# A decoder layer on one core: P3 summed onto P5, block-transposed norm roots, and a separate pool for the gate operand

## The chip, the cores and the metric

The kernel runs on one core of a Trainium2 chip. The metric is the time of one execution in microseconds (us) on the device, as the median of several runs. Engines are named as the profile names them: PE is TensorE's matmul (PEld its weight load), DVE VectorE, ACT ScalarE, POOL GpSimd, SP SyncE, whose queue issues most transfers.

## The reference

One decoder layer, batch 1, 1024 tokens of 1024 features, all in fp32:

```python
z = rms_norm(h, norm_mix_g)            # n0
proj = z @ w_in                        # pool, LRU and gate channels
h = h + concat(pool_mixer, rg_lru * gelu(gate)) @ w_out
z = rms_norm(h, norm_mlp_g)            # n1
h = h + square(relu(z @ w_up)) @ w_down        # 4096 hidden
z = rms_norm(h, norm_ple_g)            # n2
gate = sigmoid(z @ w_ple_gate + b_ple_gate)
h = h + gate * (p @ w_ple_proj)        # p: 256 features
return rms_norm(h, norm_final_g)       # fin
```

## The kernel before, in words

**Layout and precision.** Activations lie transposed: features on the 128 partitions, tokens along the row. A tile of 128x1024 is one block of 128 features. A product of fp32 accuracy is made of three matmuls: each operand is split into an upper part (a cast to `float32r`, on ACT, line 153) and a lower part (the value less the upper part, on DVE, line 154; with a norm gain lines 156 and 157), and `mm` (line 321) issues upper x upper, upper x lower and lower x upper into one PSUM bank. So every weight tile goes through a load, an ACT cast and a DVE subtraction before its matmuls, and one weight pair of tiles (`wu_0` ... `wu_3`, `wd_P_0` ... in the rows) is made while another is used.

**Stages.** Up to 155 us: first norm, input projection, mixers and gates. To 242: output projection (`ps_o`). To 557: MLP up (`ps_P_u`), 16 pairs of row blocks; the two blocks of a pair and the two halves of the tokens form a 2x2 block product that is done in seven products P1 to P7 in place of eight; POOL and DVE make the sums of weights that these need (lines 183 and 186), DVE adds the results (`add`, line 652). To 863: MLP down (`ps_P_d`) in the same way, 14 products of four quarters q. Then the gated embedding: a gate product (`ps_e`, 24 matmuls a tile) and a projection of p (`ps_j`, 6 matmuls) for eight feature tiles and three token groups, 0 to 511, 512 to 767 and 768 to 1023, and the final norm of each group with its store.

**Norms.** A norm adds up squares on DVE (line 355) into an accumulator. `sums` splits that into two parts on DVE (cast line 367, subtraction line 368, tile `hl` or `ple`), and a matmul with a matrix of ones adds over partitions, so each partition of `n_ps` holds the sums for all tokens. `roots` takes the square root of it on ACT (line 384), and a DVE reciprocal of 128x512 follows (line 402; for n1 lines 749 and 754, inside pair 1). `rstd_fast`, used in the final norm only, transposes 32x32 blocks on DVE instead (line 391), takes the root and the reciprocal of the few distinct values (128x16 or 128x8, lines 395 and 396), and transposes back (line 397). n1 belongs to the first up pair, `up_first`, in which P6, P7, P4 and P5 run before P1, P2 and P3; its `sums` stand at P3. The gain by R is applied in `finish_up` (line 665), one pair late. n2 belongs to the last products of MLP down (P5, P3); its sums and the splits of the gate operand Z (line 157, tile `ple`) are made around 854 to 864.

**What sets the order.** The code is written in one sequence; a scheduler reorders instructions of each engine, except those wrapped in `pin`, which keep program order. Tiles come from pools that are opened and closed by `space` and `leave`; a tile in a pool's place waits for all users of the pool before. PSUM products alternate between a pool `pd` of single banks and `pp` of double ones (`turn` counts). Loads are issued on SP's queue in order, except that of the input projection's first weight tile (`wl`, k = 0), which is on ACT's.

**The end.** In the last group of 256 tokens the last tile's product is followed by a sigmoid (ACT, line 933), a multiplication (DVE, line 941), an addition (942), a square (1010), the ones-matmul (379), the root and reciprocal between transpositions, seven multiplications and one scaling of 128x256 (lines 964 and 968), and four stores of two tiles each. `outT` has a row of 1024 tokens per feature, so a packet of these stores holds 256 tokens.

Of the kernel before, what the change touches and what calls it, by code (L numbers as in the profile page):

```python
# [12 lines left out]
P = 128  # L13
# [10 lines left out]
LAST_POOL = ()  # L24
# [26 lines left out]
def block_kernel(  # L51
# [14 lines left out]
    outT: bass.AP,  # L66
# [193 lines left out]
    def down_step(c, kind, q):  # L260
# [22 lines left out]
        (load_weights, w_lru[k * P : (k + 1) * P, :], f"wl{k}", 3 * P, None, nc.sync if k else nc.scalar)  # L283
# [27 lines left out]
    def mm(parts, whi, wlo, zhi, zlo, first, last, only=None):  # L311
# [7 lines left out]
        for w, z in ((whi, zhi), (whi, zlo), (wlo, zhi)):  # L319
            for hs, ps in outs:  # L320
                nc.tensor.matmul(  # L321
                    ps, w, z[:, hs],
                    start=first and z is zhi and w is whi,
                    stop=last and w is wlo,
                )

# [13 lines left out]
    class Norm:  # L340


        def __init__(self, name, acc, tmp, eng=None, late=()):
            self.name, self.acc, self.tmp, self.late = name, acc, tmp, late
# [13 lines left out]
        def sums(self, halves=HALVES):  # L358

            parts = []  # L360
            for hs in halves:
                n = hs.stop - hs.start
                j = (hs.start // HALF) % 2
                hi, lo = hl(2 * j)[:, :n], hl(2 * j + 1)[:, :n]
                o = bank(f"{self.name}_ps{hs.start}")[:, :n]
                in_order[:] = self.late
                pin(nc.vector.tensor_copy(hi, self.acc[:, hs]))
                pin(nc.vector.tensor_tensor(lo, self.acc[:, hs], f32(hi), ALU.subtract))
# [13 lines left out]
        def roots(self, out, parts):  # L382
            for hs, o in parts:
                nc.scalar.activation(out[:, hs], o, AF.Sqrt, bias=eps, scale=1.0 / D)

        def rstd_fast(self, out, parts):


            for hs, o in parts:
# [213 lines left out]
    norm = Norm("n1", T[4], T[5:], late=[True])  # L603
# [41 lines left out]
    def product(ps, w, operand, ts=range(4), n=4):  # L645
        (whi, wlo) = w
        for t in ts:
            zhi, zlo = operand(t)
            mm([(FIRST, ps)], kblk(whi, t), kblk(wlo, t), zhi, zlo, t == 0, t == n - 1)
# [49 lines left out]
    def up_first():  # L699
# [388 lines left out]
```

## Time and profile before

| | |
|---|---|
| median of 3 runs | 990.07 us (989.76 to 990.35) |
| profiled execution | 988.36 us, span 986.5 us |
| instructions | 11505, matmuls 4472 |
| PE busy | 968.2 us (98%) |
| DVE, ACT, POOL busy | 775.0, 445.8, 100.4 us |
| granted TensorE clock | 0.995 of full speed over the span |

A row of the timeline starts with its start in us from the start of the span and its duration, then the engine, the line of the kernel, the operation, output and inputs, the shape and how many such rows are merged; in brackets stands the engine's idle time before it and what ended that. In a stretch of time (A:B) stand busy times with counts in the order PE, PEld, DVE, ACT, POOL, then the granted clock, the share of DMA engines in use and GB/s.

### The profile page before, as it was taken

The page shows a single profiled execution, that of the slowest core. Times are in us where ns is not written, and L with a number is a line of the kernel's source. Part 1 is how long each engine was busy: PE and PEld are TensorE (multiplying, and loading weights), DVE is VectorE, ACT ScalarE, POOL GpSimd, SP SyncE. Part 2 cuts the span into 40 slices and gives each one's busy share as a digit, 9 for nine tenths or more (in the row PEclk, how much of TensorE's full clock was granted, in tenths as well). Part 3 has the DMA queues.
Part 4 walks back from the last instruction along what each step waited for, and adds up shares of the span by engine and source line. Part 5 has one row for each costly group of instructions (what it writes and reads, how often), then busy time and mean ns, then how long its engine had stood idle before and what let it go on. Part 6 is the DMA issues. An engine that isn't in the chain of part 4 may idle for free.

```text
span 986.5 us, 11505 instructions
## 1 busy us (share of the span) xinstructions
PE 968.2 (98%) x4472; PEld 805.6 (82%) x4472; DVE 775.0 (79%) x883; ACT 445.8 (45%) x526; POOL 100.4 (10%) x72
## 2 busy tenths in 40 slices
PE   9999999999899999999999999999999999999996
PEld 7888888888677888888888888888888888878995
DVE  7999994459896777767767889879775668795976
ACT  8368743347333334333433444344343335653544
POOL 0000000002522332232232000000000000000110
PEclk9999999999999999999999999999999999999998
DMA  6210243112124533543543897356533331131122
GB/s 223 88 44 33 86 150 107 44 43 71 47 108 155 196 118 139 199 133 126 175 169 118 293 359 261 132 174 208 175 117 95 107 106 44 43 111 61 44 86 86
DMA packets 46710, 125.04 MB, mean 127 GB/s; under 512 B 5312, under 2 KB 8384, under 8 KB 46656
## 3 DMA queue, kind: packets, MB, share of 16 engines
q1 hardware_dynamic: 46368, 124.08, 36.8%
q8 instruction: 35, 0.57, 0.2%
q10 hardware_dynamic: 288, 0.24, 0.1%
q14 instruction: 19, 0.16, 0.0%
HBM read 90.74 MB, written 33.55 MB: 126 GB/s over the span
## 4 chain that ended last, share of the span: by engine, by line
PE 84%; DVE 9%; ACT 3%; DMA 1%; issue 1%; SPq 1%; POOL 1%; DVEq 0%; ACTq 0%; POOLq 0%
PE ps_P_d L321 30%; PE ps_P_u L321 28%; PE ps_i L321 10%; PE ps_o L321 8%; PE ps_e L321 5%; PE ps_l L321 1%; PE ps_g L321 1%; DVE t L355 1%; DVE h L942 1%; DVE h L955 1%; DVE wu_lo L154 1%; DVE y L157 1%; DVE t L941 1%; SPq L419 1%; DMA h<-in_xT 1%
## 5 line engine op out<-in xcount | busy, mean ns | idle before, releaser
L321 PE MATMUL ps_P_d<-a,wd_P_hi 128*128 128x512 f32 x880 | 271.0, 389 | 0.0
L321 PEld LDWEIGHTS ps_P_d<-a,wd_P_hi 128*128 128x128 f32 x880 | 165.2, 188 | 34.5
L321 PE MATMUL ps_P_d<-a,wd_P_lo 128*128 128x512 f32 x440 | 171.3, 389 | 0.0
L321 PE MATMUL ps_P_u<-a,wu_hi 128*128 128x512 f32 x512 | 157.7, 389 | 0.0
L321 PE MATMUL ps_P_u<-y,wu_hi 128*128 128x512 f32 x384 | 119.1, 392 | 0.0
L321 PEld LDWEIGHTS ps_P_u<-a,wu_hi 128*128 128x128 f32 x512 | 96.1, 188 | 20.0
L652 DVE TENSOR_TENSOR t<-t,ps_P_u 128x512 f32<-128x512 f32 (+1 forms) x84 | 65.1, 779 | 46.5 <-PE ps_P_u L321 45.8
L321 PE MATMUL ps_P_u<-a,wu_lo 128*128 128x512 f32 x256 | 99.6, 389 | 0.0
L321 PEld LDWEIGHTS ps_P_d<-a,wd_P_lo 128*128 128x128 f32 x440 | 82.6, 188 | 17.3 <-DVE wd_P_lo L154 0.3
L321 PEld LDWEIGHTS ps_P_u<-y,wu_hi 128*128 128x128 f32 x384 | 72.6, 189 | 15.2 <-ACT wu_hi L153 0.2
L321 PE MATMUL ps_P_u<-y,wu_lo 128*128 128x512 f32 x192 | 75.3, 393 | 3.4 <-DVE wu_lo L154 3.4
L321 PE MATMUL ps_i<-a,wi_hi 128*128 128x512 f32 x288 | 77.5, 390 | 0.0
L154 DVE TENSOR_TENSOR a<-wd,a 128x1024 fp32r<-128x1024 f32 x56 | 67.1, 1219 | 6.4 <-ACT a L153 5.3
L153 ACT ACTIVATE a<-wd 128x1024 fp32r<-128x1024 f32 x56 | 58.8, 1057 | 22.3 <-PE ps_P_d L321 11.8
L321 PE MATMUL ps_o<-y,wo_hi 128*128 128x512 f32 x256 | 68.4, 389 | 0.0
L321 PEld LDWEIGHTS ps_i<-a,wi_hi 128*128 128x128 f32 x288 | 53.9, 188 | 11.5 <-ACT h L520 0.5
L153 ACT ACTIVATE wu_hi<-wu 128x1024 fp32r<-128x1024 f32 x24 | 25.5, 1062 | 82.9 <-PE ps_P_u L321 45.8
L153 ACT ACTIVATE wu_hi<-wu_raw 128x1024 fp32r<-128x1024 f32 (+1 forms) x25 | 25.3, 1010 | 74.9 <-PE ps_P_u L321 37.5
L321 PEld LDWEIGHTS ps_o<-y,wo_hi 128*128 128x128 f32 x256 | 48.0, 188 | 10.0
L321 PEld LDWEIGHTS ps_P_u<-a,wu_lo 128*128 128x128 f32 x256 | 48.0, 188 | 10.0
L154 POOL TENSOR_TENSOR wg_lo<-wg_raw,wg_hi 128x1024 fp32r<-128x1024 f32 x4 | 9.7, 2436 | 410.3 <-ACT wg_hi L153 410.3
L153 ACT ACTIVATE wd_P_hi<-wd 128x1024 fp32r<-128x1024 f32 x24 | 25.4, 1059 | 56.4 <-PE ps_P_d L321 56.2
(225 smaller groups left out, 1655.8 us busy)
## 6 DMA issues: line engine op xcount, KB each, us to landing
wd<-act SPq DMA_DIRECT2D x56, 512.0 KB, 5.6
act<-t SPq DMA_DIRECT2D x32, 512.0 KB, 3.9
wu_raw<-in_w_up SPq DMA_DIRECT2D x16, 512.0 KB, 4.2
wu<-in_w_up SPq DMA_DIRECT2D x16, 512.0 KB, 4.2
act<-wu SPq DMA_DIRECT2D x16, 512.0 KB, 4.2
wd<-in_w_down SPq DMA_DIRECT2D x16, 512.0 KB, 6.2
h<-in_xT SPq DMA_DIRECT2D x15, 512.0 KB, 4.5
wg_raw<-in_w_gate SPq DMA_DIRECT2D x12, 512.0 KB, 3.3
```

Of the source, the lines that this page charges most:

```text
L153: pin(nc.scalar.activation(hi, src, AF.Copy))
L154: pin((eng or nc.vector).tensor_tensor(lo, src, f32(hi), ALU.subtract))
L157: pin(nc.vector.scalar_tensor_tensor(lo, src, g, f32(hi), ALU.mult, ALU.subtract))
L321: nc.tensor.matmul(ps, w, z[:, hs], start=first and z is zhi and w is whi, stop=last and w is wlo,)
L355: self.eng.tensor_tensor(self.acc[:, hs], self.acc[:, hs], sq, ALU.add)
L419: nc.sync.dma_start(rv[r, pair, a, :, r], gates[pair, a, par])
L652: (eng or nc.vector).tensor_tensor(to, to if y is None else y, x, ALU.add)
L941: nc.vector.tensor_tensor(e, t, pj, ALU.mult)
L942: nc.vector.tensor_tensor(hv, hv, e, ALU.add)
L955: nc.vector.scalar_tensor_tensor(hv, hv, col("g_fin", o), rfin[:, hs], ALU.mult, ALU.mult)
```

## The change

1. `up_first`: P3 is summed in PSUM onto the bank that holds P5 (`more=True`: no start flag), after ACT has copied P5 to `s`. The additions on DVE are regrouped: six instead of nine.
2. n1's split is made right after that copy: upper parts on ACT, lower ones on DVE, pinned (`casts`); the four ones-matmuls follow P3 without a product between them.
3. `rstd` is now what `rstd_fast` was, for all norms; the 128x512 reciprocals are gone.
4. `open_down`/`open_ple`/`open_proj`: the second group of down weight tiles has a pool of its own, so that the pool of the gate operand Z can open in P5; the projection's operands have a pool `proj`, and `w_proj` is loaded right behind p on SP's queue. n2's first half is cast at P3 and summed after the first gate.
5. The load of the input projection's first weight tile goes to SP's queue as the others do. In SP's new order the load of the sixth (k = 5) stands ahead of eight small loads (`in_gates`), behind which it stood before.
6. The end: the last tile gets two single PSUM banks; its sigmoid comes before the square and gain of the tile before it; the last two gains are done on ACT; four multiplications of 128x512 write to T[1:3], and the output of the last 256 tokens is stored apart, contiguous in each partition, and put together on the host.

```diff
-        (load_weights, w_lru[k * P : (k + 1) * P, :], f"wl{k}", 3 * P, None, nc.sync if k else nc.scalar)
+        (load_weights, w_lru[k * P : (k + 1) * P, :], f"wl{k}", 3 * P)
...
+        def casts(self, halves=HALVES):
+            for hs in halves:
+                hi, lo = self.parts(hs)
+                nc.scalar.activation(hi, self.acc[:, hs], AF.Copy)
+                ins = nc.vector.tensor_tensor(lo, self.acc[:, hs], f32(hi), ALU.subtract)
+                tc.keep_in_program_order(ins)
...
+        def rstd(self, out, parts=None):
+            for hs, o in parts or self.sums():
                 r = out[:, hs]
                 nc.vector.transpose(r, o)
...
-        def rstd(self, out, parts=None):
-            for hs, o in parts or self.sums():
-                self.roots(out, [(hs, o)])
-                nc.vector.reciprocal(out[:, hs], out[:, hs])
...
-        copy(s, ps["P6"])
-        add(c22, ps["P7"], s)
-        add(c21, ps["P4"], c22)
-        add(c22, ps["P5"])
-        add(c12, ps["P5"], s)
+        copy(s, ps["P5"])
+        norm.casts()
...
+        for kind in ("P1", "P2"):
+            ps[kind] = mlp_bank(f"ps_{kind}_u0")
+            product(ps[kind], ws[kind], lambda t, kind=kind: up_operand(kind, t))
+        product(ps["P5"], ws["P3"], lambda t: up_operand("P3", t), more=True)
+        parts = norm.sums(cast=True)
+        copy(c11, ps["P1"])
+        add(c12, ps["P6"], c11)
+        add(c22, ps["P7"], c12)
+        add(c11, ps["P2"])
+        add(c21, ps["P4"], c22)
+        add(c22, s)
+        add(c12, ps["P5"])
+        norm.rstd(R, parts)
...
-            nc.vector.reciprocal(R[:, FIRST], R[:, FIRST])
...
-            nc.vector.reciprocal(R[:, SECOND], R[:, SECOND])
...
-        tiles = space("wd", 12, F32)
+        tiles = space("wd", 8, F32)
+        late = space("wd1", 4, F32, "right")
...
-        tiles = space("ple", 14, F32R)
+        tiles = space("ple", 10, F32R)
...
+        leave("wd1")
         leave("wu")
-        B[2:4] = pairs(space("proj", 4, F32R, "right"))
+        B[:4] = pairs(space("proj", 8, F32R, "right"))
...
                 if n == 0:
+                    first_sums()
                     continue
...
-        for n, o in enumerate(tiles):
-            hv = H[o][:, hs]
-            eng = nc.gpsimd if n in LAST_POOL else nc.vector
-            eng.tensor_tensor(hv, hv, rfin[:, hs], ALU.mult)
+        gain(end, hs)
+        done = t_all[:, 1:3].rearrange("p a (b s) -> p (a b) s", s=hs.stop - hs.start)
+        r = rfin[:, hs].unsqueeze(1).broadcast_to([P, 2, hs.stop - hs.start])
+        low = end // 2 * 2
+        for o in [*(o for o in range(0, NT, 2) if o != low), low]:
+            os = slice(o, o + 2)
+            nc.vector.tensor_tensor(done[:, os], h_all[:, os, hs], r, ALU.mult)
+            nc.sync.dma_start(out_end[:, os], done[:, os])
```

The scheduler decides what these edits do to each engine's order. Three places show it. The first is DVE's queue around the end of `up_first` and the start of pair 1. `hl` is n1's split, `wu_k_lo` the lower part of the up weights' k-th tile, `t<-t,ps_P_u` an addition of a product's result. Before:

```order
L154 TENSOR_TENSOR wu_3_lo<-wu_0_raw,wu_3_hi 128x512
L652 TENSOR_TENSOR t<-t,ps_P_u_1851 128x512 x3
L652 TENSOR_TENSOR t<-t,ps_P_u_1868 128x512
L154 TENSOR_TENSOR wu_0_lo<-wu_1745,wu_0_hi 128x1024
L367 CAST hl_135<-t 128x512
L368 TENSOR_TENSOR hl_135<-t,hl_135 128x512
L367 CAST hl_136<-t 128x512
L652 TENSOR_TENSOR t<-t,ps_P_u_1882 128x512
L368 TENSOR_TENSOR hl_136<-t,hl_136 128x512
L154 TENSOR_TENSOR wu_1_lo<-wu_1745,wu_1_hi 128x1024
L749 RECIPROCAL rstd<-rstd 128x512
L652 TENSOR_TENSOR t<-t,ps_P_u_1932 128x512
```

And now, from the weight part whose product was late at 254.44 (`wu_2_lo`; before, two additions stood ahead of it):

```order
L153 TENSOR_TENSOR wu_2_lo<-wu_0_raw,wu_2_hi 128x1024
L371 TENSOR_TENSOR hl_135<-t,hl_135 128x512
L371 TENSOR_TENSOR hl_136<-t,hl_136 128x512
L153 TENSOR_TENSOR wu_3_lo<-wu_0_raw,wu_3_hi 128x512
L659 TENSOR_TENSOR t<-t,ps_P_u_1783 128x512
L659 TENSOR_TENSOR t<-t,ps_P_u_1793 128x512
L659 TENSOR_TENSOR t<-t,ps_P_u_1808 128x512
L659 TENSOR_TENSOR t<-t,ps_P_u_1868 128x512
L153 TENSOR_TENSOR wu_0_lo<-wu_1749,wu_0_hi 128x1024
L659 TENSOR_TENSOR t<-t 128x512
L659 TENSOR_TENSOR t<-t,ps_P_u_1818 128x512
L402 STREAM_TRANSPOSE rstd<-n_ps_1893 128x512
```

The lower parts of `hl` have moved ahead of all additions, and no cast of the upper parts is left on DVE. Behind these rows follow a second transposition, pair 1's `wu_1_lo`, two reciprocals of 128x16, two transpositions back, the scaling of `up_first`'s result (128x2048), an addition and pair 1's `wu_2_lo`.

The second place is PE at the start of the gated embedding, where n2's sums (`n_ps`) stand. Before, where `ps_P_d_3` is the last down product:

```order
L321 MATMUL ps_P_d_3_5900<-a,wd_P_3_lo 128x512
L321 MATMUL ps_e_0_5939<-ple_5690,wg_0_hi 128x512
L321 MATMUL ps_e_0_5939<-ple_5691,wg_0_hi 128x512
L321 MATMUL ps_e_2_6029<-ple_5698,proj_5930 128x512
L321 MATMUL ps_e_2_6029<-ple_5699,proj_5930 128x512
L370 MATMUL n_ps_5887<-ple_5688,ones 128x512
L321 MATMUL ps_e_1_5970<-ple_5690,wg_1_hi 128x512
```

And now, at the end of the first gate's 24 matmuls:

```order
L320 MATMUL ps_e_0_5942<-ple_5704,wg_0_hi 128x512
L320 MATMUL ps_e_0_5942<-ple_5703,wg_0_lo 128x512
L384 MATMUL n_ps_5974<-ple_5705,ones 128x512
L385 MATMUL n_ps_5974<-ple_5705,ones 128x512
L320 MATMUL ps_e_1_5981<-ple_5697,wg_1_hi 128x512
L320 MATMUL ps_e_1_5981<-ple_5698,wg_1_hi 128x512
```

The lower part's sum came four matmuls into the embedding; both sums now come after a whole gate. DVE's splits of the gate operand, eight in a row before, now stand among the weight parts of the last P5 and P3 products: four, three and one between one part and the next.

The third is ACT at the end, from the last but one sigmoid (`ps_e_2`) on. Before:

```order
L933 ACTIVATE t<-ps_e_2_6913,vecs 128x256
L1012 ACTIVATE t<-h 128x256
L1015 ACTIVATE h<-h,vecs 128x256
L933 ACTIVATE t<-ps_e_3_6955,vecs 128x256
L939 ACT_TABLE_LOAD
L939 ACTIVATE root<-t 128x1
L395 ACTIVATE edge<-t,eps 128x8
```

And now:

```order
L944 ACTIVATE t<-ps_e_2_6925,vecs 128x256
L944 ACTIVATE t<-ps_e_3_6966,vecs 128x256
L1030 ACTIVATE t<-h 128x256
L1031 ACT_TABLE_LOAD
L1031 ACTIVATE root<-t 128x1
L973 ACTIVATE h<-h,vecs 128x256 x2
L406 ACTIVATE edge<-t,eps 128x8
```

The last sigmoid has moved ahead of the square, and two gains now stand between the table load and the root.

More of the change, by code (lines that the diff above doesn't have):

```diff
@@ L309, in small_weights, with mm @@
         return hi, lo
-    def mm(parts, whi, wlo, zhi, zlo, first, last, only=None):
+    def mm(parts, whi, wlo, zhi, zlo, first, last, only=None, more=False, held=False):
         outs = [
@@ L600, in block_kernel @@
     gate_out(3, project(8))
-    norm = Norm("n1", T[4], T[5:], late=[True])
+    norm = Norm("n1", T[4], T[5:])
     for o in range(NT):
@@ L643, in mlp_bank, with product @@
         return banks(name)[:, :HALF] if len(turn) % 3 == 0 else bank(name)
-    def product(ps, w, operand, ts=range(4), n=4):
+    def product(ps, w, operand, ts=range(4), n=4, more=False):
         (whi, wlo) = w
@@ L648, in product @@
             zhi, zlo = operand(t)
-            mm([(FIRST, ps)], kblk(whi, t), kblk(wlo, t), zhi, zlo, t == 0, t == n - 1)
+            mm([(FIRST, ps)], kblk(whi, t), kblk(wlo, t), zhi, zlo, t == 0 and not more, t == n - 1, more=more)
     def add(to, x, y=None, eng=None):
@@ L868, in down @@
                 if (kind, q) == ("P3", 2):
-                    norm2.rstd(R, norm2.sums((FIRST,)))
+                    norm2.casts((FIRST,))
     Z, ple = [], []
@@ L899, in block_kernel, with first_sums @@
     open_proj()
+    def first_sums(norm=norm2):
+        norm.rstd(R, norm.sums((FIRST,), cast=True))
     norm2 = Norm("n2b", T[0], T[1:3])
@@ L936, in ple_out @@
             nc.scalar.activation(t, t, AF.Sigmoid, bias=col("b_ple", o))
-        if last:
-            nc.scalar.activation(root, t[:, :1], AF.Sqrt)
-        e = T[3 + (o + last) % 2][:, : hs.stop - hs.start]
+        e = t
+        if then:
+            then(t)
+            e = T[3 + (o + 1) % 2][:, : hs.stop - hs.start]
         nc.vector.tensor_tensor(e, t, pj, ALU.mult)
@@ L951, in finish @@
     def finish(hs):
-        fin.rstd_fast(rfin, fin.sums((hs,)))
+        fin.rstd(rfin, fin.sums((hs,)))
         for o in range(NT):
```

137 lines of the change are left out of this document (66 added, 71 removed).

## The prediction, made before the changed kernel had run

> **What bounds the kernel now.** I read the page's busy times and the chain of waits first, then what TensorE waits for, then the stretches around those waits.
>
> ```profile
> PE 968.2 (98%) x4472; PEld 805.6 (82%) x4472; DVE 775.0 (79%) x883; ACT 445.8 (45%) x526; POOL 100.4 (10%) x72
> PE 84%; DVE 9%; ACT 3%; DMA 1%; issue 1%; SPq 1%; POOL 1%; DVEq 0%; ACTq 0%; POOLq 0%
> ```
> ```profile
> PE ps_P_u L321 <- DVE wu_lo L154: 3.4, 4, 1.6
> PE n_ps L369 <- DVE hl L367: 1.8, 2, 0.9
> PE n_ps L379 <- DVE t L1010: 1.6, 1, 1.6
> ```
> ```profile
> 570.00:860.00 290.00, 290.00 (x1281) 239.84 (x1280) 226.23 (x230) 127.08 (x138) 0.00 (x0) 1.00 0.45 151
> ```
> The first line is busy time by engine, the second the shares of the chain that ended last: TensorE sets the time nearly everywhere. The third to fifth (who waited for whom: total, times, longest) put nearly all of its waits on VectorE (DVE). The last is a stretch of time with the busy time of PE, weight loads, DVE, ACT and POOL: TensorE is never idle there, and 1281 matmuls of 512 columns in 290.00 us are one per 0.2264 us, which I round to 0.227; a 256-column one takes half, 0.1135. A delay is measured below from start to start against this spacing, because the records' ends overlap. The change leaves the matmuls' number as it is, so all it can win is such delays and the tail after the last matmul.
>
> **The norm sums in the first up pair.** TensorE's and DVE's rows at n1:
>
> ```profile
> 261.64 0.39 PE L321 MATMUL ps_P_u<-y,wu_lo 128*128 128x512 f32 x1
> 262.95 0.50 PE L369 MATMUL n_ps<-hl,ones 128*128 128x512 f32 x1 [0.92 <-DVE hl L367]
> 264.62 0.50 PE L370 MATMUL n_ps<-hl,ones 128*128 128x512 f32 x1 [1.17 <-DVE hl L368]
> ...
> 269.39 0.62 PE L321 MATMUL ps_P_u<-y,wu_hi 128*128 128x512 f32 x2
> ```
> ```profile
> 261.36 1.53 DVE L367 CAST hl<-t 128x512 fp32r<-128x512 f32 x1
> 262.93 1.64 DVE L368 TENSOR_TENSOR hl<-t,hl 128x512 fp32r<-128x512 f32 x1
> ...
> 863.34 0.68 DVE L368 TENSOR_TENSOR ple<-t,ple 128x512 fp32r<-128x512 f32 x1
> ```
> ```profile
> 263.00:267.00 4.00, 1.91 (x4) 1.15 (x5) 4.00 (x4) 0.00 (x0) 3.92 (x3) 0.84 0.00 0
> 265.70:269.20 3.50, 3.16 (x8) 2.51 (x9) 2.93 (x4) 2.03 (x2) 1.34 (x1) 0.51 0.00 0
> ```
> From 261.64 to 269.39 eleven matmuls start: 7.75 - 11 x 0.227 = 5.25 us lost. Three gaps (0.92, 1.17, and 0.9 more of the 1.8 that L369 waits in all; 3.0 together) are waits for casts that stand behind weight work in DVE's queue; the rest is the half clock that followed (granted clock 0.51 in the second stretch). The casts ran slow, 1.53 and 1.64 where the same subtraction later takes 0.68, while POOL was busy (3.92 of 4.00 us in the first stretch).
>
> The change casts right after P5 leaves PSUM, while all of P1, P2 and P3 (36 matmuls, 8.2 us) are still ahead of the sums. ACT makes both upper parts, DVE both lower ones straight after the third weight's:
>
> ```profile
> 257.08 0.60 ACT L684 ACTIVATE t<-ps_P_u 128x512 f32<-128x512 f32 x1 [0.65 <-PE ps_P_u L321]
> ```
> P5 ends by about 254, when the next weight's matmuls begin (the rows at 252.64 and 254.44 below); a copy and two casts on ACT at 0.60 and two subtractions at the slow 1.64 put the last near 259 even if none overlap, against a need at 261.4 with the earlier gain. So 36 matmuls hide it with 2 us to spare: **-5.25**.
>
> **The weight waits in the first pairs.**
>
> ```profile
> 252.64 1.07 PE L321 MATMUL ps_P_u<-y,wu_hi 128*128 128x512 f32 x4
> 254.44 0.50 PE L321 MATMUL ps_P_u<-y,wu_lo 128*128 128x512 f32 x1 [0.74 <-DVE wu_lo L154]
> ...
> 289.27 0.50 PE L321 MATMUL ps_P_u<-y,wu_lo 128*128 128x512 f32 x1 [1.56 <-DVE wu_lo L154]
> ```
> ```profile
> 251.79 1.47 DVE L652 TENSOR_TENSOR t<-t,ps_P_u 128x512 f32<-128x512 f32 x2
> ...
> 257.71 2.48 DVE L652 TENSOR_TENSOR t<-t,ps_P_u 128x512 f32<-128x512 f32 x4 [0.56 <-ACT t L684]
> ...
> 270.24 3.35 DVE L749 RECIPROCAL rstd<-rstd 128x512 f32<-128x512 f32 x1 [0.77 <-ACT rstd L384]
> ...
> 274.37 3.35 DVE L754 RECIPROCAL rstd<-rstd 128x512 f32<-128x512 f32 x1
> ...
> 291.17 3.27 DVE L665 SCALAR_TENSOR_TENSOR t<-t,rstd 128x2048 f32<-128x2048 f32 x1
> ```
> The matmul at 254.44 is late by 1.80 - 4 x 0.227 = 0.89. Its lower weight part stood behind two additions in DVE's queue (1.47 us) that the change puts later. That is more than was missing; but POOL runs across 251.39 to 253.01 in its stead:
>
> ```profile
> 251.39 1.62 POOL L186 TENSOR_TENSOR wu<-wu,wu 128x512 f32<-128x512 f32 x1
> ```
> Bounds 0 (the subtraction slowed by as much as the casts above, some 1 us) and -0.9; I take **-0.6**, since the L652 pair beside that POOL row lost only 0.2. The Trainium skill has a rule against it: in "SBUF — State Buffer", section "Who interferes with whom", a DVE operation with two SBUF inputs and a GpSimd one that reads SBUF exclude each other for the whole instruction. By it the subtraction would start at 253.0 and the wait would stay, a sum smaller by 0.6; the casts' rows agree with the rule.
>
> Of the 3.4 us that wu_lo's four waits sum to, 3.4 - 0.74 = 2.7 are left for three later ones; at 254.44 the start-to-start loss is a fifth above the idle time (0.89 to 0.74), so 3.2 to 3.3. DVE was behind by its own queue: two reciprocals (6.70), nine P-additions in the first pair where six now do (3 x 0.62 = 1.9), and two casts that go to ACT. It gets four block transpositions and two 128x16 reciprocals instead:
>
> ```profile
> L397 DVE STREAM_TRANSPOSE t<-edge 128x512 f32<-128x512 f32 x1 | 0.7, 711 | 0.0
> ```
> 4 x 0.71 = 2.8 and about 0.5 make DVE some 6.7 to 8.3 us lighter before 282, over twice the 2.7 that was missing; pair 2's second weight part also stands ahead of the 3.27 us scaling in the new queue. Summing P3 onto P5 in PSUM costs TensorE nothing, since it writes the same count of columns. Bounds -1.5 (a wait comes back, first rival) and -3.3; I take **-3.0**.
>
> **The gated embedding's start, and one release in it.**
>
> ```profile
> 863.15 0.61 PE L321 MATMUL ps_e<-ple,proj 128*128 128x512 f32 x2
> 864.08 0.50 PE L370 MATMUL n_ps<-ple,ones 128*128 128x512 f32 x1 [0.31 <-DVE ple L368]
> 864.72 0.73 PE L321 MATMUL ps_e<-ple,wg_hi 128*128 128x512 f32 x2
> ```
> ```profile
> 837.13 1.22 DVE L154 TENSOR_TENSOR wd_P_lo<-wd,wd_P_hi 128x1024 fp32r<-128x1024 f32 x1
> ...
> 840.89 1.22 DVE L652 TENSOR_TENSOR h<-h,ps_P_d 128x1024 f32<-128x1024 f32 x1 [0.33 <-PE ps_P_d L321]
> ...
> 857.44 5.38 DVE L157 SCALAR_TENSOR_TENSOR ple<-h,vecs,ple 128x512 fp32r<-128x512 f32 x8
> ```
> ```profile
> 944.63 0.50 PE L321 MATMUL ps_e<-a,wg_hi 128*128 128x256 f32 x2 [0.35 <-DVE t L941]
> ```
> 863.15 to 864.72 holds three matmuls: 1.57 - 0.68 = 0.89 lost, behind eight gate-operand splits in DVE's queue. With a pool of their own they run in the last P5 and P3 products, four, three and one of them between one weight part and the next, and the sums follow a whole gate of 24 matmuls (5.4 us): **-0.9** (-0.7 to -0.9). What hides the splits there is that the weight part made from 837.13 to 838.35 is first used after 840.89, when the product before it ends: 2.5 us of slack. In the fullest product DVE has an addition and a weight part (1.22 each), four splits (5.38 / 8 = 0.67 each) and a norm addition (0.68), 5.8 us in 5.45, so it falls back by some 0.4, and by 1.1 over three: the slack holds. The 0.35 at 944.63 is a PSUM release behind DVE's final scaling; the last norm's reciprocals, before it in the queue, become short. **-0.3**, bounds 0 and -0.35.
>
> **Start, first norm, tail.**
>
> ```profile
> 17.31 6.25 SPq L419 DMA_DIRECT2D t<-in_gates  x8
> ...
> 26.89 1.19 PE L321 MATMUL ps_l<-a,wl_hi 128*128 128x512 f32 x4 [0.20 <-ACT wl_hi L153]
> ```
> ```profile
> 974.53 0.87 PE L321 MATMUL ps_j<-ple,proj 128*128 128x256 f32 x6
> ...
> 976.01 0.46 ACT L933 ACTIVATE t<-ps_e,vecs 128x256 f32<-128x256 f32 x1
> ...
> 976.50 0.42 DVE L941 TENSOR_TENSOR t<-t,ps_j 128x256 f32<-128x256 f32 x1 [1.39 <-ACT t L933]
> ...
> 980.17 2.44 DVE L964 TENSOR_TENSOR h<-h,t 128x256 f32<-128x256 f32 x7
> 982.52 0.48 DVE L968 SCALAR_TENSOR_TENSOR h<-h,vecs,t 128x256 f32<-128x256 f32 x1
> ```
> The weight load that the matmul at 26.89 needs is issued after eight small loads (6.25 us of SP's queue). It now stands ahead of them: 0.20 to win, and SP carries one more load early, which can delay the blocks of h behind it by one issue; **-0.2**, bounds +0.3 and -0.2. The first norm's two reciprocals become transpositions too; no wait of TensorE's in the list names them, so 0. In the tail the last sigmoid stands behind another tile's square and gain on ACT. Put first, it lets the multiplication start when the projection ends (974.53 + 0.87 = 975.40) and not at 976.50: 1.10, less 0.05 for the releases, with ACT's square, table load and gains now under DVE's and TensorE's next steps. Four doubled multiplications (2.48 for such four at 257.71) replace 983.00 - 980.17 = 2.83: -0.35. Together **-1.4**, bounds -1.0 and -1.8 (larger store packets, for which no row has a price).
>
> **Sum.** 5.25 + 0.6 + 3.0 + 0.9 + 0.3 + 0.2 + 1.4 = 11.65. The profiled execution took 988.36 (span 986.5 and 1.86 around it), so its like would take 976.7; the timed median, 990.07, lies 1.71 above it, and the forecast for the median is 990.07 - 11.65 = **978.4**. With 5.25 kept, the other bounds sum to -8.15 (5.25 + 0 + 1.5 + 0.7 + 0 - 0.3 + 1.0) and -12.7 (5.25 + 0.9 + 3.3 + 0.9 + 0.35 + 0.2 + 1.8): 977.4 to 981.9.
>
> **Rivals.**
> *A wait comes back in pair 1.* After the sums DVE must do transpositions (1.4), pair 1's second weight part (1.2), reciprocals and transpositions behind ACT's roots (to 4.8), the scaling (2.3 to 3.3) and an addition before the third weight part (1.2), some 10 to 10.5 us; TensorE needs it 48 matmuls and two on, 11.3. Against it: about 1 us is free. For it: POOL beside DVE, as at 262.93. All of the -3.0 lost: 981.4. Chance 0.17.
> *The casts stay late*, so that the change doesn't do what it says: POOL holds them up and two of the three gaps remain, 0.92 + 1.17, with the half clock's 5.25 - 3.00 = 2.25: 978.4 + 4.3 = 982.7. For it: the slow rows; against it: 2 us to spare. Chance 0.07. The Trainium skill, "TensorE: Matmul & The Clock Gate", section "What's actually happening", has the clock halved only after an idle window of about 3.4 us; by it this rival would be 980.5. The trace decides: it fell after gaps of at most 1.17.
> *Slower:* DVE falls back further among those last products, because each of the eight lower parts waits for its upper part from ACT, which also squares there. From a loss of 11.65 + 2 = 13.65 us this is slower than before. Eight waits of 1.2 (an ACT operation of 0.60 and a square of like length) and the 1.1 above, less the slack of 2.5, are 8.2 us of missing weights; in three products the clock would fall each time, 3 x 2.25 = 6.8, together 15.0: 993.4. Against it: DVE is busy 226.23 and ACT 127.08 of 290 us there, so ACT is nowhere near full. Chance 0.03.
>
> **Chances and range.** Forecast 0.70, the first two rivals 0.24, slower 0.03, and 0.03 that several smaller mishaps leave no more than 0.2% of gain (about 2 us, what a measurement of this kernel can tell): faster 0.94, same 0.03, slower 0.03. Range 975.5 to 982.9: the bounds and both rivals above, and 1.9 below 977.4 because the profiled execution, from which the terms come, lies 1.7 under the median.
>
> **What would show it.** Right: no n_ps wait and a clock of 1.00 from 255 to 275; no wait for wu_lo from 280 to 320; n_ps after a full gate without idle; the last multiplication within 0.1 us of the last projection. Wrong: wu_lo waits over 0.5 us in pairs 1 to 3, subtractions of over 2 us beside POOL, waits for wd_P_lo from 820 to 863, or ACT's gain ending after the last transposition.

## The result, and the profile after

The changed kernel takes 977.38 us (976.44 to 977.87) against 989.91 us before, a ratio of 0.9873 with a 95% interval of 0.9856 to 0.989. The forecast was 978.4. In the two profiled executions the span fell from 986.5 to 975.5, by 11.0, of the 11.65 that the terms summed to.

The page's busy times and chain shares of the changed kernel, then what its TensorE waits for (total, times, longest; the 1.3 us at the very start, the same in both kernels, is left out):

```profile
PE 964.8 (99%) x4472; PEld 805.2 (83%) x4472; DVE 757.0 (78%) x885; ACT 442.7 (45%) x528; POOL 99.1 (10%) x72
PE 95%; DVE 3%; ACT 1%; DMA 1%; issue 0%; SPq 0%; DVEq 0%
```
```profile
PE n_ps L394 <- DVE t L1037: 0.6, 1, 0.6
PE ps_P_u L320 <- DVE wu_lo L153: 0.4, 1, 0.4
PE ps_l L320 <- DVE a L156: 0.3, 1, 0.3
PE ps_e L320 <- DVE t L952: 0.3, 1, 0.3
```
DVE's share of the chain fell from 9% to 3%. Of the waits on `hl` none is left, and of the four on `wu_lo` one.

**n1.** The four ones-matmuls, and two stretches with their granted clock (the third number from the end):

```profile
261.67 0.40 PE L384 MATMUL n_ps<-hl,ones 128*128 128x512 f32 x1
...
262.37 0.39 PE L385 MATMUL n_ps<-hl,ones 128*128 128x512 f32 x1
```
```profile
255.00:275.00 20.00, 20.00 (x90) 16.50 (x89) 16.95 (x22) 9.73 (x13) 7.32 (x5) 1.00 0.26 86
280.00:320.00 40.00, 40.00 (x177) 32.79 (x176) 29.81 (x29) 13.59 (x16) 12.13 (x10) 1.00 0.42 150
```
Four sums start within 0.70 us, one matmul's spacing apart. By its records TensorE is busy for all of both stretches, and the clock stays at 1.00. One sign of being wrong did appear, a subtraction of over 2 us beside POOL:

```profile
279.85 1.28 POOL L185 TENSOR_TENSOR wu<-wu,wu 128x512 f32<-128x512 f32 x1
280.02 2.20 DVE L153 TENSOR_TENSOR wu_lo<-wu_raw,wu_hi 128x1024 fp32r<-128x1024 f32 x1 [0.18 <-ACT wu_hi L152]
```
It cost little: the two matmuls ahead start at 281.67 and the one that needs it at 282.27, 0.60 - 0.45 = 0.15 us late.

**The late weight part at 254**, over PE, ACT, DVE and POOL:

```profile
248.21 1.14 ACT L370 ACTIVATE hl<-t 128x512 fp32r<-128x512 f32 x2
251.38 1.07 ACT L152 ACTIVATE wu_hi<-wu_raw 128x1024 fp32r<-128x1024 f32 x1 [2.03 <-PE ps_P_u L320]
251.52 1.62 POOL L185 TENSOR_TENSOR wu<-wu,wu 128x512 f32<-128x512 f32 x1
252.48 1.75 DVE L153 TENSOR_TENSOR wu_lo<-wu_raw,wu_hi 128x1024 fp32r<-128x1024 f32 x1 [0.48 <-ACT wu_hi L152]
252.76 1.07 PE L320 MATMUL ps_P_u<-y,wu_hi 128*128 128x512 f32 x4
254.15 2.38 DVE L371 TENSOR_TENSOR hl<-t,hl 128x512 fp32r<-128x512 f32 x2
254.28 0.50 PE L320 MATMUL ps_P_u<-y,wu_lo 128*128 128x512 f32 x1 [0.45 <-DVE wu_lo L153]
```
The upper casts of `hl` came even earlier than I said, at 248.21, as soon as the sum of squares was there; the lower ones are done at 256.53, 5 us ahead of their use. But DVE, now free of the two additions, idles 0.48 us for ACT's upper part of the weight, which itself waited 2.03 us for TensorE; and then its subtraction takes 1.75 us where others of its size take 1.22. TensorE's loss went from 0.89 to 254.28 - 252.76 - 0.91 = 0.61 only.

**The start and the end.**

```profile
11.40 0.73 PE L320 MATMUL ps_l<-a,wl_hi 128*128 128x512 f32 x2 [0.31 <-DVE a L156]
```
```profile
965.00 0.87 PE L320 MATMUL ps_j<-proj,proj 128*128 128x256 f32 x6
...
965.20 0.47 ACT L944 ACTIVATE t<-ps_e,vecs 128x256 f32<-128x256 f32 x1 [1.21 <-PE ps_e L320]
...
965.96 0.42 DVE L952 TENSOR_TENSOR t<-t,ps_j 128x256 f32<-128x256 f32 x1 [1.06 <-PE ps_j L320]
```
```profile
969.62 2.50 DVE L984 TENSOR_TENSOR t<-h,t 128x512 f32<-128x512 f32 x4
```
Three marks cut the program where the same matmuls stand in both kernels: the four of 252.64 and 252.76, and the last projection's six.

| stretch | before | after | difference | predicted |
|---|---|---|---|---|
| to the four matmuls ahead of 254 | 252.64 | 252.76 | +0.12 | -0.2 |
| from there to the last projection | 721.89 | 712.24 | -9.65 | -10.05 |
| last projection to the span's end | 11.97 | 10.50 | -1.47 | -1.4 |

### The profile page after: what moved, and what is told of

Read it like the earlier page. It is cut to its first block, busy times and chain, and to the rows that moved or that the text cites. A ratio compares the mean times of both kernels' runs of the same rounds, so it can differ in the third digit from the quotient of the medians.

```text
span 975.5 us, 11507 instructions
## 1 busy us (share of the span) xinstructions
PE 964.8 (99%) x4472; PEld 805.2 (83%) x4472; DVE 757.0 (78%) x885; ACT 442.7 (45%) x528; POOL 99.1 (10%) x72
## 4 chain that ended last, share of the span: by engine, by line
PE 95%; DVE 3%; ACT 1%; DMA 1%; issue 0%; SPq 0%; DVEq 0%
PE ps_P_u L320 31%; PE ps_P_d L320 31%; PE ps_i L320 10%; PE ps_o L320 9%; PE ps_e L320 8%; PE ps_l L320 3%; PE ps_g L320 1%; PE ps_j L320 1%; PE ps_p L320 1%; DVE h L968 1%; DMA h<-in_xT 1%; DVE a L153 1%; DVE a L156 0%; DVE t L984 0%; DVE wu_lo L153 0%
## 5 line engine op out<-in xcount | busy, mean ns | idle before, releaser
L659 DVE TENSOR_TENSOR t<-t,ps_P_u 128x512 f32<-128x512 f32 (+1 forms) x80 | 62.6, 784 | 47.9 <-PE ps_P_u L320 47.7
```

What stands on the lines that cost most here:

```text
L659: (eng or nc.vector).tensor_tensor(to, to if y is None else y, x, ALU.add)
```

## Experiments

Times move by about 1 us from one execution of the same kernel to the next, so the spans of repeated executions and the waits in the traces carry the small differences. The changed kernel's spans were 974.5 to 975.8, those of the kernel before 986.0 to 988.0 in three further series.

**Casts late again (undo one part).** The split of n1 goes back to P3, on DVE, pinned:

```diff
-        norm.casts()
...
+                if cast is None:   # n1, at P3
+                    pin(nc.vector.tensor_copy(hi, self.acc[:, hs]))
+                    pin(nc.vector.tensor_tensor(lo, self.acc[:, hs], f32(hi), ALU.subtract))
```

> The changed kernel with one part undone: n1's split stands again at P3, both parts on DVE, cast and subtraction pinned behind the weight parts, as in the kernel before; P3 on P5, the block-transposed roots and all else stay. My theory: the early place of the casts is what took away the 5.25 us at n1, so TensorE waits for hl again, 2 to 3 us in two to four waits, the granted clock falls below 1 for about 3.4 us behind them, and the span grows from 975.5 by 3.5 to 5.5, to 979 to 981. Rival: the stall went because DVE has fewer additions and no long reciprocals, and the casts would be in time at their old place too: no n_ps wait over 0.5 us, clock 1.00, span 975.0 to 976.3.

Measured: 981.73 us (ratio to the kernel before 0.993, 0.9915 to 0.9945), spans 979.3 to 980.1. TensorE's waits:

```profile
PE n_ps L388 <- DVE hl L383: 1.9, 1, 1.9
...
PE n_ps L387 <- DVE hl L382: 0.7, 1, 0.7
```
Two waits come back, and the half clock behind them (0.50 of full speed from 266.20 to 269.60); the span grows by some 4 to 5 us. The early place of the casts is the cause, and the rival falls. Why it is a little less than 5.25 was not shown.

**Reciprocals back in n1 (undo one part).**

```diff
-        norm.rstd(R, parts)
+        for hs, o in parts:
+            nc.scalar.activation(R[:, hs], o, AF.Sqrt, bias=eps, scale=1.0 / D)
+        for hs, o in parts:
+            nc.vector.reciprocal(R[:, hs], R[:, hs])
```

> The changed kernel with one part undone: n1's reciprocal root is again a square root of 128x512 on ACT and a DVE reciprocal of 128x512 for each half; the early casts and all else stay. My theory: the two reciprocals (6.7 us) are what made the weight parts of pairs 1 and 2 late, so waits for wu_lo come back between 262 and 320, 2.5 to 6 us in all, and the span grows to 978 to 982. Rival: the later waits were an echo of the stall at n1 and of the order of POOL's and SP's work, which this kernel keeps as changed: at most 0.5 us of wu_lo waits behind 262 and a span of 975.0 to 976.3.

Measured: 978.16 us (0.9894, 0.9879 to 0.9909), spans 975.9 to 976.4, about 1 us over the changed kernel. The wait on `wu_lo`, and the DVE row behind it:

```profile
PE ps_P_u L320 <- DVE wu_lo L153: 1.3, 3, 0.5
```
```profile
263.10 6.56 DVE L736 RECIPROCAL rstd<-rstd 128x512 f32<-128x512 f32 x2 [0.48 <-ACT rstd L734]
```
6.56 us of DVE's queue cost TensorE only 0.9 us more of waits. My theory, which asked for 2.5 to 6, is wrong; the rival, with 0.5 at most, came nearer.

**One part alone: casts, root, and both in the kernel before.** The first adds the early casts to the kernel before, the second the root between block transpositions for n1, the third both; nothing else. The lines of the third (`casts` itself is as in the change, and `sums` no longer splits for n1):

```diff
         copy(s, ps["P6"])
+        norm.casts()
...
-                norm.roots(R, norm.sums())
+                norm.rstd_fast(R, norm.sums())
...
-            nc.vector.reciprocal(R[:, FIRST], R[:, FIRST])
...
-            nc.vector.reciprocal(R[:, SECOND], R[:, SECOND])
```

> The kernel before with one part of the change alone: n1's split is made early, upper parts on ACT and lower ones on DVE, pinned right behind P6's copy; the sums, P3's own bank, the 128x512 reciprocals and all else as before. My theory after the first runs (casts late: 4.6 of the 5.25 us at n1 came back; reciprocals back: only 1.4 more of wu_lo waits): the early casts alone take away the n1 waits and the half clock, and because DVE's queue behind them is planned anew, most of the later wu_lo waits too: span 986.5 - 5.25 - (0 to 2) = 979.3 to 981.3, time 981 to 983.5. Rival, my prediction's own step: the later waits belong to the reciprocals, so after 262 they stay at 2.7 us or more and the span is 981.0 to 982.0. Both would show a clock of 1.00 at n1; a remaining n_ps wait over 0.5 us would speak against the casts' place as the cause.

> The kernel before with another part alone: n1's root is made between block transpositions, without the two 128x512 reciprocals; casts late, P3's own bank and all else as before. If the reciprocals are what made the later weight parts late (my prediction), the wu_lo waits behind 280 fall from 2.7 us to 0.5 or less, n1's 5.25 us stay: span 983.0 to 983.8. If the waits belong to the order of the queue (additions, scaling, POOL's sums), at least 1.2 us of them stay: span 984.5 to 986.5.

> The kernel before with the two parts at n1 together and nothing else: early casts and the root between block transpositions. Alone they moved the span from 986.5 (986.0 to 988.0 in repeated runs) to 978.7 and 983.8. If the gains overlap as the traces say (either one alone takes most of the later wu_lo waits), together they give little more than the casts alone: 0.8 us more, span 977.4 to 978.4, with wu_lo waits of 0.3 or less behind 260 and the 0.9 at 254 as before. If they add, 986.5 - 7.8 - 2.7 = 976.0. The rest to the changed kernel's 975.5, about 2.5, would be the embedding (0.9), the end (1.4) and the start.

| kernel | time, ratio to before (interval) | spans |
|---|---|---|
| casts alone | 980.96, 0.992 (0.9904 to 0.9936) | 977.8 to 979.9 |
| root alone | 985.56, 0.9964 (0.9951 to 0.9978) | 982.2 to 984.2 |
| both | 981.3, 0.9923 (0.9908 to 0.9938) | 979.4 to 980.8 |

TensorE's waits on `wu_lo` with the casts alone, with the root alone, and with both:

```profile
PE ps_P_u L321 <- DVE wu_lo L154: 1.0, 2, 0.7
```
```profile
PE ps_P_u L321 <- DVE wu_lo L154: 0.7, 1, 0.7
```
```profile
PE ps_P_u L321 <- DVE wu_lo L154: 2.2, 4, 0.8
```
The 0.7 (0.8 with both) is the one at 254 in each. With the root alone no other is left: the three later waits are gone, and n1's stay. But with the casts alone the later waits nearly vanish too (0.3 is left), though the reciprocals are there. And with both there are three later waits, 1.4 us in all, at 269.69, 275.78 and 290.48: the third expectation fell, by which both together were to be 0.8 better than the casts. Where the first of them comes from, over POOL, ACT, DVE and PE of the run with both, and behind it DVE's row of the changed kernel:

```profile
262.21 1.32 POOL L186 TENSOR_TENSOR t<-wu_raw 128x512 f32<-128x512 f32 x1 [5.89 <-DVE wu_lo L154]
...
265.98 1.30 POOL L186 TENSOR_TENSOR wu<-wu 128x512 f32<-128x512 f32 x1
267.31 1.06 ACT L153 ACTIVATE wu_hi<-wu 128x1024 fp32r<-128x1024 f32 x1 [7.00 <-POOL wu L186]
268.41 1.23 DVE L154 TENSOR_TENSOR wu_lo<-wu,wu_hi 128x1024 fp32r<-128x1024 f32 x1 [4.30 <-ACT wu_hi L153]
269.69 0.50 PE L321 MATMUL ps_P_u<-y,wu_lo 128*128 128x512 f32 x1 [0.53 <-DVE wu_lo L154]
```
```profile
265.63 1.23 DVE L153 TENSOR_TENSOR wu_lo<-wu,wu_hi 128x1024 fp32r<-128x1024 f32 x1 [1.83 <-ACT wu_hi L152]
```
DVE's queue is not what is late here: DVE idles 4.30 us for ACT's cast, and that waits 7.00 us for POOL. POOL makes sums of pair 2 (`wu_raw`) ahead of the last one that pair 1's second weight part needs (`wu`), and is done with that at 267.28. In the changed kernel it makes pair 1's sums first and is done at 263.21 + 1.30 = 264.51. ACT's table load for the root, the reciprocals and the scaling follow that cast, so the third weight part, needed at 275.78, is late in its turn; at 290.48 DVE again idles 2.27 us for an ACT cast that waited for POOL. In the kernel before POOL's sum came as late (265.77 + 1.34 = 267.11) and cost nothing, because TensorE stood some 5 us behind after its stall at n1. So the stall at n1 hid POOL's order, and taking it away laid it bare.

**P3 in a bank of its own (undo one part).**

```diff
-        product(ps["P5"], ws["P3"], lambda t: up_operand("P3", t), more=True)
+        ps["P3"] = mlp_bank("ps_P3_u0")
+        product(ps["P3"], ws["P3"], lambda t: up_operand("P3", t))
...
-        add(c12, ps["P5"])
+        add(c12, s)
+        add(c12, ps["P3"])
```

> The changed kernel with P3 of the first pair in a PSUM bank of its own again, and one more addition on DVE for it (t from P5's copy, then P3's bank); casts early, transposed roots and all else stay. My theory: summing P3 in PSUM frees 0.6 us of DVE, which has idle time there (1.83 us ahead of the weight part at 265.6), so it is worth nothing: span within 0.4 of the changed kernel's 975.5, no n_ps wait. Rival: the freed bank or addition is what lets pair 1 run without waits: wu_lo waits of 0.5 us or more between 262 and 300, span over 976.0.

Measured: 976.45 us (0.9877, 0.9861 to 0.9892), spans 973.8 to 975.4, no `n_ps` wait at n1 and no `wu_lo` wait but the one at 254. Summing P3 onto P5, the first half of the change's first item, is worth nothing that can be told by itself. POOL's order is that of the changed kernel here too (pair 1's sum is done at 264.28). So of the change at n1 the regrouped additions are left as what gives POOL, ACT and DVE the order in which "both" works; they were not run by themselves.

**POOL's subtraction moved away.** A block of pair 1's weights is made later by POOL, from blocks that stand by then:

```diff
-            gp(ALU.subtract, a21, a11, a21)          # step 0
+            if m > 1:
+                gp(ALU.subtract, a21, a11, a21)
...
+            if m == 1:                               # step 1, a11 is now s1 - a11
+                gp(ALU.subtract, a21, a22, a11)
```

> The changed kernel with one of POOL's subtractions, which makes a block of pair 1's weights, moved from 251.5 (beside the lower weight part that is late at 254.3) to behind that pair's other sums near 264; it is worked out as a22 less the new a11, which is the same block but for rounding. If POOL and DVE exclude each other in SBUF (the rule that I weighed in the prediction), DVE's 128x1024 subtraction at 252.5 takes 1.22 us and not 1.75, and the wait of 0.4 us at 254.3 shrinks to 0.1 or less: span 975.0 or a little under. If the subtraction is slow for another reason, or the wait is set by ACT's cast alone, it still takes 1.5 us or more and the span stays at 975.4 to 975.8. In both cases the later POOL work could make pair 1's third weight part late, which would show as a wait near 272.

Measured: 976.68 us (0.9878, 0.9861 to 0.9894), spans 974.2 to 975.3. The subtraction and the matmul that needs it:

```profile
252.17 1.22 DVE L153 TENSOR_TENSOR wu_lo<-wu_raw,wu_hi 128x1024 fp32r<-128x1024 f32 x1 [0.48 <-ACT wu_hi L152]
```
```profile
252.46 1.07 PE L323 MATMUL ps_P_u<-y,wu_hi 128*128 128x512 f32 x4
253.44 0.50 PE L323 MATMUL ps_P_u<-y,wu_lo 128*128 128x512 f32 x1
```
With POOL silent the same subtraction takes 1.22 and not 1.75 us, and TensorE loses 253.44 - 252.46 - 0.91 = 0.07 and not 0.61. The rule of the Trainium skill ("SBUF — State Buffer", "Who interferes with whom") holds: in the changed kernel DVE's subtraction ends at 254.23, 1.09 after POOL's end at 253.14, though it started at 252.48. No wait near 272 came of it. The 0.5 us is too little to tell in the time, and this execution lost 0.6 us at 552.95, on a wait of MLP down for DVE that is 0.2 in the changed kernel.

**The first weight load on ACT's queue**, alone and together with POOL's moved subtraction:

```diff
-        (load_weights, w_lru[k * P : (k + 1) * P, :], f"wl{k}", 3 * P)
+        (load_weights, w_lru[k * P : (k + 1) * P, :], f"wl{k}", 3 * P, None, nc.sync if k else nc.scalar)
```

> The changed kernel with two things bettered: POOL's subtraction of pair 1 moved away from the late weight part (alone it cut TensorE's loss at 254 from 0.72 to 0.19), and the input projection's first weight load on ACT's queue again. My theory: on SP's queue that load puts off the blocks of h behind it, which cost 0.4 at 8.5 and 0.6 at 11.4 us of the changed kernel and won 0.6 at 26.9 and 67.8; on ACT's queue the start loses 0.2 us less, the two together 0.5 to 0.8: span 974.7 to 975.0, time under the changed kernel's by 0.5 to 0.8. Rival: the start's loss belongs to the first weight's late cast and not to the queue, so it stays above 3.0 us up to 70 us, and only the 0.5 at 254 is won: span 975.0.

> The changed kernel with the input projection's first weight load on ACT's queue again, and nothing else. Together with POOL's moved subtraction this won 0.7 us up to 27 us and lost 1.4 at 67, where a gate's matmuls waited for DVE. If that wait belongs to this load's place (TensorE comes earlier, DVE's scaling of ps_i, planned anew, later), it is here too, 0.8 to 1.4 us, and the span is 975.2 to 976.2. If it came from the moved subtraction, there is none and the span is 973.8 to 974.8.

Measured: together 977.13 us (0.9884, 0.9867 to 0.9902), alone 977.76 us (0.9883, 0.9867 to 0.99), spans 975.0 to 975.7 and 975.6 to 976.2. Neither can be told from the changed kernel by its time. (The 0.72 and 0.19 in the first of the two expectations are the losses of 0.61 and 0.07, counted to one matmul further on.) With the load alone, the wait, the matmuls and the DVE row that they wait for, and behind them the two rows of the changed kernel:

```profile
PE ps_g L320 <- DVE t L489: 0.8, 1, 0.8
```
```profile
66.08 1.22 DVE L489 TENSOR_TENSOR t<-ps_i,rstd 128x1024 f32<-128x1024 f32 x1
...
67.35 1.65 PE L320 MATMUL ps_g<-y,hl 128*128 128x512 f32 x6 [0.79 <-DVE t L489]
```
```profile
65.17 1.22 DVE L489 TENSOR_TENSOR t<-ps_i,rstd 128x1024 f32<-128x1024 f32 x1
...
66.67 1.52 PE L320 MATMUL ps_g<-y,hl 128*128 128x512 f32 x6
```
In the changed kernel DVE's scaling frees a bank at 66.39 and the matmuls start at 66.67: 0.3 us to spare. On ACT's queue the load lets TensorE reach the gate's first matmuls 0.27 us earlier (62.10 against 62.37) and DVE's scaling comes 0.9 later. So the place of this load decides 0.8 us far behind it, and by the traces it is better where the change put it.

**The sums ahead of the first gate, and one pool for the down weights (each undoes half of one part).**

```diff
-                ple_gate(g, hs, o, pg, n == 1)
+                if n == 0:
+                    first_sums()
+                ple_gate(g, hs, o, pg, n == 0)
...
-                    first_sums()
```
```diff
-        tiles = space("wd", 8, F32)
-        late = space("wd1", 4, F32, "right")
+        tiles = space("wd", 12, F32)
+        late = tiles[2 * NQ :]
...
-        leave("wd1")
```

> The changed kernel with n2's two ones-matmuls ahead of the first gate's 24 matmuls and not behind them; the split of n2 and of the gate operand stay as changed. In the changed kernel the lower part of the split is done at 851.1 and the embedding starts at 853.8. If the 0.89 us at 864 went because the gate operand's splits left DVE's queue there (one half of my reason), nothing is lost: span 975.3 to 975.8. If the place of the sums behind a whole gate matters (the other half), TensorE waits there again 0.3 to 1.0 us: span 975.8 to 976.5.

> The changed kernel with the down weights in one pool of 12 tiles again, so that the gate operand's pool opens only when all of them are read: the eight lower parts of the operand stand in one piece in DVE's queue, ahead of the lower part of n2's split and of the first gate weight's; the sums stay behind the first gate. The run with the sums ahead of that gate lost nothing, so the other half of my reason should carry the 0.89 us: I expect TensorE to wait at the start of the embedding (854 to 860 us) for a DVE result, 0.5 to 2.5 us in all, span 975.5 to 977.5. Rival: with the sums behind a gate either place of the splits is hidden, no wait over 0.2 us there, span 974.3 to 975.5.

Measured: 976.45 us (0.9881, 0.9866 to 0.9896) with the sums ahead, 977.03 us (0.9876, 0.9862 to 0.9891) with one pool, where the eight splits stand in one piece again; spans 974.4 to 976.3 and 974.4 to 975.7. In both traces TensorE loses nothing between 853 and 860. My expectation for the second was wrong. The first run shows that the sums may stand at the gate's start once the splits are out of the way. The second says less than I meant it to, because it does not bring back the place that the splits had: in the kernel before DVE made p's lower parts (2.35 us, at 855.17) ahead of the eight splits, which so ended at 857.44 + 5.38 = 862.82, behind the embedding's start at 862.70; here p's come later, and the eight end at 845.38 + 5.39 = 850.77, ahead of the start at 853.12. So late splits with the sums behind a whole gate were not tried, and p's later place may be a third part of what removed the 0.89 us.

**The last sigmoid behind the square and gain again.**

```diff
-                    pin(nc.scalar.activation(sqs[0], H[prev][:, hs], AF.Square))
                     pin(nc.scalar.activation(root, t[:, :1], AF.Sqrt))
-                    pin(gain(prev, hs))

                 in_order[:] = [True]
+                pin(nc.scalar.activation(sqs[0], H[prev][:, hs], AF.Square))
+                pin(gain(prev, hs))
                 ple_out(hs, o, pg, pj, False, between)
```

> The changed kernel with the last sigmoid behind the square and the gain of the tile before it on ACT, as in the kernel before; the doubled multiplications and the stores stay as changed. My theory: of the 1.4 us at the end, 1.0 belong to the sigmoid's place and the rest to four multiplications for eight, so the last multiplication starts about 1.0 us after the last projection's end (now 0.1), TensorE's last wait grows from 0.62 to about 1.6, and the span from its usual 974.1 to 975.5 to 975.1 to 976.5. Rival: ACT's table load, which now follows, sets the end, so that the order of sigmoid and square moves the end by 0.3 or less.

Measured: 977.24 us (0.9881, 0.9867 to 0.9896), spans 975.2 to 976.2.

```profile
964.41 0.87 PE L320 MATMUL ps_j<-proj,proj 128*128 128x256 f32 x6
...
964.81 0.51 ACT L973 ACTIVATE h<-h,vecs 128x256 f32<-128x256 f32 x1
965.23 0.46 ACT L944 ACTIVATE t<-ps_e,vecs 128x256 f32<-128x256 f32 x1
...
965.72 0.42 DVE L952 TENSOR_TENSOR t<-t,ps_j 128x256 f32<-128x256 f32 x1 [1.39 <-PE n_ps L394]
```
The sigmoid stands behind the gain again, and the last multiplication starts 965.72 - 964.41 = 1.31 us after the projection's start: 0.96 in the changed kernel, 1.97 before. So the order gives 0.35 of the 1.01, where I asked for 1.0 and the rival for 0.3 or less. The other 0.66 is there without it: the square and the gain of the tile before come earlier in relation to TensorE than they did. The trace leads that back to DVE's eight scalings of the middle token group, behind which sigmoid, multiplication, addition, square and gain follow at 2.27 us a tile in both kernels: they start at 964.80 before and 954.60 now, 9.73 and 10.40 us ahead of the last projection. Why they start earlier was not tried.

## Why the prediction was right, point by point

- **n1, -5.25: right, with its cause.** The loss went to nothing, and with late casts most of it came back. One detail was wrong without effect: the casts wait for the sum of squares and not for P5.
- **254, -0.6: mis-sized, 0.28.** The step that failed is that the weight part stood behind two additions. It did, but without them it waits for ACT's cast and then for POOL. The moved subtraction shows the second: -0.54 more. The rule of the Trainium skill's "SBUF — State Buffer", which gave 0 here, was the better guide to the cause; the measured value lies between.
- **The later waits, -3.0: the size was right, the cause told too simply, and in part that is luck.** The stretch between the marks leaves 9.65 - 5.25 - 0.28 - 0.89 - 0.08 = 3.15, which holds all else that changed there. I put all three waits down to DVE's queue. Those at 289.27 and 295.63 stood behind it; before the third, at 315.52 (0.53 us), DVE had idled 2.28 us for an ACT cast that waited for POOL. The root alone removes all three, but putting the reciprocals back into the changed kernel cost 0.9 and not 3, and casts and root together brought 1.4 of waits through POOL's order, which the prediction does not mention for these waits; its first rival, a wait that comes back in pair 1, came about in that kernel, by another path than the one it gave. The term holds for the whole of the change in this place, not for the reciprocals.
- **The embedding's start, -0.9: right in size**, 0.89 gone. Of the two reasons given as one, the place of the sums is not needed; the place of the splits, and of p's before them, was not put back.
- **944, -0.3: 0.08.** The release is still late: 0.27 idle of 0.35. The step that failed is that the last norm's reciprocals become short: they were short before (128x16, 0.25 us at 936.31, ahead of the scaling at 937.53), so nothing ahead of DVE's scaling was to become shorter.
- **Start, -0.2: +0.12, the wrong sign, within its bounds.** What I set against it, blocks of h put off by one issue, is what happened: ACT waits 1.92 us for one and splits it from 6.97 (5.64 before), and the 0.31 at 11.40 follows. In the runs with that load back on ACT's queue the start was faster, and a matmul 40 us on then waited for DVE.
- **First norm, 0: right, by 0.3 us.** I gave no margin for it, and the runs with the load moved show that there is next to none.
- **Tail, -1.4: right in size**, -1.47; the sigmoid's place carries 0.35 and not 1.05 of it, the doubled multiplications and stores 0.46 (10.50 - 0.96 = 9.54 us from the last multiplication's start to the end, 11.97 - 1.97 = 10.00 before).
- **Profiled execution and median.** I set the terms against 990.07, as if both kernels' profiled executions lay 1.71 under their medians. The changed kernel's own was 977.54 at a median of 977.38. 988.36 less the measured 11.0 is 977.4. So the trace's gain fell short of the terms by 0.65, while the median fell by 1.5 us more than the trace, which brought the forecast out 1.0 too high. That the two errors go against each other is luck. The kernel before took 988.71 to 989.46 (medians) in the three later series and 989.91 in this one, so 0.5 to 1.2 of the 1.5 lies within what its times vary by from series to series.
- **The rivals** did not come about: no `hl` wait, one `wu_lo` delay behind 254 that is too small for the list (the 0.15 at 282.27), and TensorE busy for all of the stretch from 820 to 863:

```profile
820.00:863.00 43.00, 43.00 (x192) 35.55 (x191) 36.60 (x50) 27.91 (x41) 0.00 (x0) 1.00 0.07 25
```

## What to carry to other kernels

When a wait has several causes, what removing one of them gains depends on the others: try a part alone, and the whole without it, before crediting it. Here casts and root gave some 8 and 3 us alone (ratios of 0.992 and 0.9964) and no more together than the casts did (0.9923). A stall of the bounding engine hides what else is late, and once it is gone the engines behind it have that much less time. Where a weight part is late, follow it back through each of its makers (the load or buffer release, POOL's sums, the cast, the subtraction) and look at what runs beside them; that it ends on DVE does not say that DVE's queue is the cause.

## What the runs showed of the hardware

- **The half clock lasted 3.4 us in two traces and twice that in a third.** With half speed as the low state, a mean of 0.51 over 3.5 us in the kernel before is (1 - 0.51) x 3.5 / 0.5 = 3.4 us, and with the casts late it was 0.50 from 266.20 to 269.60. In the kernel with the root alone, with nearly the same waits at n1 as before:

```profile
264.00:271.50 7.50, 6.30 (x15) 4.62 (x16) 6.36 (x10) 2.99 (x4) 2.99 (x2) 0.54 0.00 0
```

 Worked out in the same way, (1 - 0.54) x 7.5 / 0.5 = 6.9 us. Whether that is why the times of the kernel before differ from one execution to the next was not shown: spans of 987.1 us stand at mean clocks of both 0.993 and 0.997. No idle gap at n1 was longer than 1.2 us in the kernel before and in that with the root alone, so the idle window of about 3.4 us of the Trainium skill ("TensorE: Matmul & The Clock Gate", "What's actually happening") is not needed for the fall: with the casts late, gaps of 1.9 and 0.7 did it too, while the single wait of 1.56 us at 289.27 in the kernel before did not (clock 1.00 from 286 to 299). The section "A second HAM failure mode: psum-queue depth-cycling" of that page of the Trainium skill tells of frequent short idles between groups of matmuls that make the clock swing; that is nearer to what stands here, but it gives no length or share of idle time to compare.
- **POOL loses to DVE as well.** DVE and POOL in the changed kernel, ahead of 254 and in n1:

```profile
247.92 2.35 DVE L153 TENSOR_TENSOR a<-t,a 128x1024 fp32r<-128x1024 f32 x2
248.14 3.31 POOL L185 TENSOR_TENSOR t<-wu 128x512 f32<-128x512 f32 x1 [16.32 <-DVE t L358]
...
262.49 1.30 DVE L402 STREAM_TRANSPOSE rstd<-n_ps 128x512 f32<-128x512 f32 x2
263.21 1.30 POOL L185 TENSOR_TENSOR wu<-wu 128x512 f32<-128x512 f32 x1
```

 A POOL operation of the same shape takes 3.31 us where DVE's two subtractions of SBUF tiles run until 250.27, and ends 1.18 after them; it takes 1.30 us where it overlaps by 0.58 with transpositions that read PSUM, and 1.32 with DVE idle (at 264.46).
